# Two-layer hybrid trunk (DeltaNet and HGRN2 heads): one triangular inverse per layer instead of one per head pair, and the HGRN2 score levels in one step

## The chip, the cores and the metric

The kernel runs on one core of one Trainium2 chip, as one launch. The metric is the device time in microseconds (us); the time before is 1264.35 us, the median of three runs (1264.16 to 1266.21). One more run was taken with the profiler: its own time is 1263.9 us and its span, from the first to the last instruction of the program, is 1262.1 us. So 1.8 us lie outside the span, and the profiled run stands 0.45 us below the median.

The engines are named as in the profile: PE is TensorE, PEld its weight loads, DVE is VectorE, ACT is ScalarE, POOL is GpSimd, SP is SyncE, which here only issues DMAs.

## The reference

The model is a trunk of two layers over 256 tokens of width 2048. Each layer norms the residual h, multiplies it by one input matrix of 8208 columns, feeds two groups of heads, multiplies their joined output by an output matrix, and adds a gated per-layer embedding:

```python
for l in range(DEPTH):
    hn = rms_norm(h, norm_w[l])
    proj = hn @ w_in[l]
    y_a = deltanet_branch(dn_qkv, dn_z, dn_b, dn_a, ...)   # 8 heads of 128
    y_b = hgrn2_branch(hg_q, hg_f, hg_i, hg_z, ...)        # 8 heads of 128
    h = h + concatenate([y_a, y_b]) @ w_out[l]
    gate = sigmoid(h @ w_ple_gate[l])
    h = h + (p[l] @ w_ple_up[l]) * gate
return rms_norm(h, final_norm_w)
```

The DeltaNet branch solves, for every head and chunk, a unit lower triangular system, which the kernel does by forming the inverse:

```python
A = where(strict, einsum("bhncd,bhnsd->bhncs", k_beta, k) * decay, 0.0)
sol = triangular_solve(A + eye, rhs, left_side=True, lower=True, unit_diagonal=True)
```

The HGRN2 branch forms causal scores with a decay for each channel, `A = einsum("bhrd,bhsd,bhrsd->bhrs", q, k, exp(G_r - G_s))`, and multiplies them into the values. The result does not depend on the chunk length; the kernel works in chunks of 128 tokens, so a head has two chunks.

## The kernel before

**The large products.** Every matrix product of the trunk is made in three passes of rounded factors: `whi` by the high part of the activations, `wlo` by the high part, `whi` by the low part (`products`, L414). A weight piece of 512 KB is loaded on SP's queue into `raw`; `prep` (L387) rounds it on ACT to `whi` (L400) and subtracts on DVE to `wlo` (L402). One *step* (`run_step`, L436) multiplies one such piece: two K tiles, two token tiles and three passes, 12 PE matmuls with 512 moving columns. Three pieces of `raw` and three of `whi`/`wlo` are held, and pieces are prepared two steps ahead (`LOOK`).

**The stages.** A layer has three stages: `in` (17 chunks of up to 512 columns), `out` (4 chunks) and `gate` (4 chunks, with `up`). `in_order` (L61) gives the chunks of `in`: `kq` is the k and q columns of one pair of DeltaNet heads (group g of four), `vz` its v and gate columns, `fq` and `iz` the forget/query and value/gate columns of a pair of HGRN2 heads. The first two chunks of a stage are taken alternately. `OUT_KTS` (L72) is the order in which `out` reads the eight results `y` (two K tiles each: 0 to 7 are DeltaNet, 8 to 15 HGRN2).

**The small work.** The heads' own work is written as generators, which are spawned when their chunk of `in` is finished. After every step `tick` (L358) counts all of them down by one; a generator that yields a number goes on that many steps later. The numbers stand in `DELAY` and `DELAY_AT` (L38 to L54): for instance `t16` 2 means that the next group of small matmuls stands two steps further on. All PE instructions keep the order in which they are written (`PEOrder`, L334), so a small matmul whose operand is late stops the large products behind it. The instructions of the other engines are ordered by a scheduler of the framework from the order of the text and the free buffers; a few DVE instructions and DMAs are pinned too.

**DeltaNet, per pair of heads (`DN`, L612).** A pair has four 128x128 matrices (two heads by two chunks). `dkdq` convolves k and q; `k_side` waits `k` steps; `q_side` waits `q` steps, makes the strict triangles `Bt` and the scores `QK` (L725 to L734), and then inverts its four matrices: it writes `Bt` to DRAM (L738), reads the 16x16 diagonal blocks back as `F` with one block to a partition, 32 partitions (L742), substitutes column by column with 30 DVE instructions (L752 to L757), writes the block inverses to the diagonal of the cleared DRAM array `d2` (L758), and reads the whole matrices back as `Tt` (L760). Three doublings follow, each with two groups of fp32 matmuls `pp` and `px`: from 16 to 32 in 64x64 blocks (L767 to L785), from 32 to 64 in 32x32 blocks (L787 to L806), from 64 to 128 in 64x64 blocks (L808 to L825). `dv` waits for this inverse (L841) and then runs a chain of small groups `pz`, `pS`, `pw`, `pz`, `po`, one step apart.

**HGRN2, per pair of heads (`HG`, L890).** The scores of a chunk are put together from levels: at level u a block of u rows meets the u columns ahead of it, with factors in which the decay is split at the block's edge (`factors`, L955). The levels go out in four groups of matmuls, three steps apart: level 1 with the diagonal and level 2 (called A below), 4 and 8 (B), 16 and 32 (C), 64 and the product of the two chunks, 128 (D). `place` (L988) merges the levels into the score tile by predicated copies.

Of the kernel before, what the change touches and what calls it, by code (L numbers as in the profile page):

```python
# [31 lines left out]
def chunk_cols(chunk):  # L32
# [6 lines left out]
    "d": {'c': 1, 'D': 4, 'k': 5, 'q': 5, 'ssq': 1, 'F': 3, 'T': 9, 't16': 2, 'p16': 2, 't32': 2, 'p32': 2, 't64': 2, 'p64': 2, 'v': 5, 'z0': 1, 'S': 1, 'w': 1, 'z1': 1, 'o': 1, 'y': 3, 'yp': 1},  # L39
    "b": {'o': 1, 'g': 4},  # L40
    "h": {'c': 1, 'f': 1, 'a': 4, 'u1': 3, 'u4': 3, 'u16': 3, 'o': 2, 'y': 2, 'yp': 1, 'q': 0},
# [30 lines left out]
OUT_KTS = (0, 1, 2, 3, 4, 5, 8, 9, 10, 11, 6, 7, 12, 13, 14, 15)  # L72
# [75 lines left out]
def const_arrays():  # L148
    i = np.arange(128)
    c = np.zeros((128, 4 * 128 + 256 + 32), np.float32)  # L150
    c[:, 0:128] = np.eye(128)
    c[:, 128:256] = 1.0
    c[:, 256:384] = i[:, None] > i[None, :]
    c[:, 384:512] = i[:, None] <= i[None, :]
    c[:, 512:768] = (np.arange(256) % 128 != 0)[None, :]
    c[:, 768:800] = i[:, None] % 32 == np.arange(32)[None, :]
    s, r = i[:, None], i[None, :]
    m = np.zeros((128, NMASK), np.int32)
    m[:, 0:32] = (s % 64 // 32 == np.arange(32)[None, :] // 16) & (s % 32 < 16)
# [7 lines left out]
def trunk(ctx: ExitStack, tc: tile.TileContext, head, xT, x, pT, W, par, fw, cst, msk, eye, out):  # L167
# [19 lines left out]
    cs = cp.tile([128, 800], F32, name="cs")  # L187
    ms = cp.tile([128, NMASK], I32, name="ms")

    def first(out, in_):  # L190
# [4 lines left out]
    xt = [mp.tile([128, 1024 if k else 1024 + NNW], F32, tag="et" if k < 2 else "kq", name=f"xt{k}", bufs=2)  # L195
          for k in range(4)]
# [73 lines left out]
    ident, ones, SL, UI = (cs[:, 128 * j:128 * j + 128] for j in range(4))  # L270
    keep, ident32 = cs[:, 512:768], cs[:, 768:800]
# [8 lines left out]
    d2 = dr.tile([66048], F32, name="d2")  # L280
    dfull = lambda d: d.rearrange("(i x) -> i x", i=4)[:, 0:16384].rearrange("i (p c) -> p i c", c=128)
    ddiag = lambda d: d.rearrange("(q x) -> q x", q=32)[:, 0:2048].rearrange("q (s f) -> q s f", s=16)[:, :, 0:16]
# [4 lines left out]
    def clear_scratch():  # L287
        V.tensor_copy(SLr, SL)
# [5 lines left out]
        tc.keep_in_program_order(nc.scalar.dma_start(out=dfull(d2), in_=zero.rearrange("p (i c) -> p i c", i=4)))  # L294
# [181 lines left out]
    def small(tag, n=4):  # L476
        return sp.tile([128, n], F32, tag=tag, name=tag)
# [133 lines left out]

    class DN:  # L612


        def __init__(self, l, g, row, y):
            self.l, self.g, self.row, self.y = l, g, row, y
# [13 lines left out]
        def decay(self):  # L630
# [17 lines left out]
            self.eG, self.neG = small("eG", 2), small("neG", 2)  # L648
# [20 lines left out]
        def conv_silu_kq(self, ps, which, w):  # L669
            ac, sg = self.conv(ps, which)  # L670
            for hh in range(2):
                V.tensor_tensor(self.kq[:, hh, :, w, :], v4(ac[:, 256 * hh:256 * hh + 256]),
                                v4(sg[:, 256 * hh:256 * hh + 256]), ALU.mult)

        def stat(self, w, name):

            ps = pm.tile([128, 512], F32, tag="m", name=self.n + name)
            for i in range(4):
                PE.transpose(ps[:, 128 * i:128 * i + 128], self.kq[:, i // 2, i % 2, w, :], ident)
# [6 lines left out]
        def dkdq(self, ps, c0):  # L686
# [4 lines left out]
            self.kq = mix("kq", 1024, 2, n + "kq").rearrange("p (h t w c) -> p h t w c", h=2, t=2, w=2)  # L691
# [5 lines left out]
        def k_side(self):  # L697
# [4 lines left out]
            self.ktail = mix("ktail", 256, 1, n + "kt")  # L702
# [4 lines left out]
            self.invn = small("invn")  # L707
            S.activation(self.invn, lk, AF.Exp, scale=0.5)
            self.b, self.nb = small("b"), small("nb")
# [6 lines left out]
        def q_side(self):  # L716
# [4 lines left out]
            Bt = self.Bt = v4(mix("Bt", 512, 1, n + "Bt"))  # L721
            self.QK = v4(mix("QK", 512, 2, n + "QK"))
            Dt = v4(self.Dt)
            for hh in range(2):
                pg = pm.tile([128, 512], F32, tag="m", name=n + f"pg{hh}")  # L725
                for t in range(2):
                    PE.matmul(pg[:, 256 * t:256 * t + 256], kq[:, hh, t, 0, :],
                              kq[:, hh, t, :, :].rearrange("p w c -> p (w c)"), start=True, stop=True)
# [10 lines left out]
            fx = tmp(n + "fx")[0:32].rearrange("q (w a b) -> q w a b", w=2, a=16)  # L739
            F, X = fx[:, 0], fx[:, 1]  # L740
            nc.scalar.dma_start(out=X, in_=eye)
            nc.scalar.dma_start(out=F, in_=ddiag(d1))  # L742
# [6 lines left out]
            self.nq = small("nq")  # L749
            S.activation(self.nq, lq, AF.Exp, scale=-0.5, bias=lnhd)  # L750
            yield self.wait("F")
# [598 lines left out]
```

## Time and profile before

| what | value |
|---|---|
| median of three runs | 1264.35 us (1264.16 to 1266.21) |
| profiled execution, its own time | 1263.9 us |
| its span | 1262.1 us |
| PE busy | 1248.5 us, 8001 matmul records |
| DVE busy | 923.6 us, 1752 instructions |
| ACT busy | 785.1 us, 1411 instructions |
| granted TensorE clock, mean | 0.997 |
| first large product starts, last one ends | 4.7 us, 1252.3 us |

An fp32 matmul stands in the trace as two records, a large product (rounded factors) as one. Because matmuls overlap in the array, a record's duration is longer than its share of the time: what a matmul costs the PE is read from the distance between starts. The timeline view merges a run of equal records into one row, which gives the start of the first.

### The profile page before, as it was taken

What the parts mean: (1) busy time and instruction counts of PE and PEld (TensorE: products, weight loads), DVE (VectorE), ACT (ScalarE), POOL (GpSimd) and SP (SyncE); (2) the same over time, 40 slices, a digit from 0 to 9 for tenths busy, and PEclk for the clock granted to TensorE, in tenths of its full rate; (3) what the DMA queues carried; (4) which work ended last, traced back from release to release, by engine and by line L of the source; (5) the groups of instructions that cost most, each with busy time, mean ns of one, the idle gap of its engine ahead of it and who ended that gap; (6) DMA issues with size and microseconds to landing.
All of it is one profiled execution on the core that took longest, in us unless ns stands there. A gap on an engine that the chain in (4) does not pass through costs nothing.

```text
span 1262.1 us, 21116 instructions
## 1 busy us (share of the span) xinstructions
PE 1248.5 (99%) x8001; PEld 1036.7 (82%) x8001; DVE 923.6 (73%) x1752; ACT 785.1 (62%) x1411; POOL 65.2 (5%) x57
## 2 busy tenths in 40 slices
PE   9999999999999999999999999999999999999996
PEld 7988887888887888888888888878888888888886
DVE  7789679787796855547668886897877968565566
ACT  7667666666666754437557677667666766444465
POOL 0100010020000000000002000100100000000010
PEclk9999999999999999999999999999999999999998
DMA  8565545455555455555555555544555545655553
GB/s 285 189 229 169 176 155 174 130 168 177 162 173 163 139 177 182 190 191 186 183 188 169 173 169 164 169 145 135 180 182 176 169 142 175 184 184 184 184 200 134
DMA packets 78246, 220.90 MB, mean 175 GB/s; under 512 B 15680, under 2 KB 25280, under 8 KB 78144
## 3 DMA queue, kind: packets, MB, share of 16 engines
q1 hardware_dynamic: 59040, 211.65, 52.2%
q10 hardware_dynamic: 19104, 7.90, 2.3%
q8 instruction: 63, 1.03, 0.3%
q14 instruction: 39, 0.32, 0.1%
HBM read 214.80 MB, written 4.72 MB: 174 GB/s over the span
## 4 chain that ended last, share of the span: by engine, by line
PE 92%; DVE 5%; ACT 1%; issue 1%; DMA 0%; SPq 0%; ACTq 0%; DVEq 0%
PE out L336 14%; PE gate L336 13%; PE in1dk L336 7%; PE in0dk L336 7%; PE in1hf L336 6%; PE in0hf L336 6%; PE in0dv L336 6%; PE in1dv L336 6%; PE in1hi L336 5%; PE in0hi L336 5%; PE up L336 2%; DVE wlo L402 1%; PE in1dz L336 1%; PE in0dz L336 1%; ACT whi L400 1%
## 5 line engine op out<-in xcount | busy, mean ns | idle before, releaser
L402 DVE TENSOR_TENSOR wlo<-raw,whi 128x1024 fp32r<-128x1024 f32 (+1 forms) x392 | 479.1, 1225 | 246.7 <-ACT whi L400 244.8
L400 ACT ACTIVATE whi<-raw 128x1024 fp32r<-128x1024 f32 (+1 forms) x392 | 411.4, 1051 | 342.2 <-PE out L336 84.2
L336 PE MATMUL in1hf<-whi,n1hi 128*128 128x512 f32 x128 | 52.5, 410 | 0.0
L336 PE MATMUL in1hi<-whi,n1hi 128*128 128x512 f32 x128 | 51.5, 403 | 0.0
L336 PE MATMUL in1dk<-whi,n1hi 128*128 128x512 f32 x128 | 51.2, 400 | 0.0
L336 PE MATMUL in1dk<-wlo,n1hi 128*128 128x512 f32 x128 | 50.0, 391 | 0.2 <-DVE wlo L402 0.2
L336 PE MATMUL gate<-whi,g0hi 128*128 128x512 f32 x128 | 50.1, 392 | 0.0
L336 PE MATMUL in1hf<-whi,n1lo 128*128 128x512 f32 x128 | 50.1, 391 | 0.0
L336 PE MATMUL in1hi<-whi,n1lo 128*128 128x512 f32 x128 | 50.0, 390 | 0.0
L336 PE MATMUL in1hf<-wlo,n1hi 128*128 128x512 f32 x128 | 49.9, 390 | 0.0
L336 PE MATMUL in1hi<-wlo,n1hi 128*128 128x512 f32 x128 | 49.9, 390 | 0.0
L336 PE MATMUL in1dk<-whi,n1lo 128*128 128x512 f32 x128 | 49.9, 390 | 0.0
L336 PE MATMUL gate<-whi,g0lo 128*128 128x512 f32 x128 | 49.8, 389 | 0.0
L336 PE MATMUL gate<-wlo,g0hi 128*128 128x512 f32 x128 | 49.8, 389 | 0.0
L336 PE MATMUL in1dv<-whi,n1hi 128*128 128x512 f32 (+1 forms) x128 | 48.3, 378 | 0.0
L336 PE MATMUL in1dv<-wlo,n1hi 128*128 128x512 f32 (+1 forms) x128 | 46.7, 364 | 0.0
L336 PE MATMUL in1dv<-whi,n1lo 128*128 128x512 f32 (+1 forms) x128 | 46.5, 363 | 0.0
L336 PE MATMUL gate<-whi,g1hi 128*128 128x512 f32 (+1 forms) x120 | 45.5, 379 | 0.0
L336 PE MATMUL gate<-wlo,g1hi 128*128 128x512 f32 (+1 forms) x120 | 45.4, 379 | 0.0
L336 PE MATMUL gate<-whi,g1lo 128*128 128x512 f32 (+1 forms) x120 | 45.4, 378 | 0.0
L336 PE MATMUL in0hf<-whi,n0hi 128*128 128x512 f32 x96 | 39.2, 408 | 0.0
L336 PE MATMUL in0hi<-whi,n0hi 128*128 128x512 f32 x96 | 38.5, 401 | 0.0
(1596 smaller groups left out, 3245.0 us busy)
## 6 DMA issues: line engine op xcount, KB each, us to landing
raw<-W SPq DMA_DIRECT2D x384, 512.0 KB, 3.5
raw<-W SPq DMA_DIRECT2D x7, 544.0 KB, 3.9
h<-x SPq DMA_DIRECT2D x4, 512.0 KB, 5.9
xt<-xT SPq DMA_DIRECT2D x3, 512.0 KB, 6.2
out_dram<-h SPq DMA_DIRECT2D x6, 256.0 KB, 2.1
fw<-fw ACTq DMA_DIRECT2D x2, 512.0 KB, 5.1
pin<-pT ACTq DMA_DIRECT2D x2, 256.0 KB, 3.2
out_dram<-h ACTq DMA_DIRECT2D x2, 256.0 KB, 2.9
```

Source lines behind the costliest of these rows:

```text
L336: return tc.keep_in_program_order(nc.tensor.matmul(*a, **k))
L400: S.activation(hi[:, sl], raw[:, sl], AF.Copy)
L402: V.tensor_tensor(lo[:, sl], raw[:, sl], hi[:, sl].bitcast(F32), ALU.subtract)
```

## The change

- `DN.q_side` ends after the q norms; its inverse moves to a new class `Inverse`, of which a layer has one. Each pair writes its `Bt` into a quarter of one large tile and into DRAM; when the fourth pair has done so, all 16 matrices of the layer are inverted together: one read of the diagonal blocks (128 partitions), 30 DVE instructions, one write, one read back, and three doublings of two groups each. The first doubling works in 32x32 blocks with 16 moving columns, where it had 64x64 blocks with 32; the second keeps its blocks; the third has its stationary operand in two halves of 32 columns.
- `in_order` takes the four `kq` chunks first; `dv` and `vz` come after the third `fq`. `OUT_KTS` starts with HGRN2's results.
- HGRN2's levels 1 to 64 go out in one group, after `f2`, `f4` and `a` steps; level 128 follows in a group of its own.
- What must outlive its pair has more buffers (`ktail`, `QK`, `eG`, `invn`, `b`, `nq`); k and q are kept in two tiles, one for each chunk. Two tiles that were loaded into `kq` are loaded into the inverse's `Tt`. The clearing of `d2` is four DMAs instead of one. The delays are set anew.

```diff
@@ q_side
-            d1 = dr.tile([66048], F32, tag="dB", name=n + "d1", bufs=2)
-            nc.scalar.dma_start(out=dfull(d1), in_=Bt)
...
-            (the inverse of four matrices, moved and widened)
+            self.inv.given(self.g)
@@ class Inverse (new)
+        def given(self, g):
+            sl = slice(4 * g, 4 * g + 4)
+            nc.scalar.dma_start(out=dfull(self.d1)[:, sl], in_=self.Bt[:, sl])
+            self.have += 1
+            if self.have == NG:
+                spawn(self.run())
+        def run(self):
+            n, Bt, NT = self.n, self.Bt, self.NT          # NT = 16
+            fx = tmp(n + "fx").rearrange("q (w a b) -> q w a b", w=2, a=16)
+            F, X = fx[:, 0], fx[:, 1]
+            nc.scalar.dma_start(out=X, in_=eye)
+            nc.scalar.dma_start(out=F, in_=ddiag(self.d1))
+            yield self.wait("F")
+            for c in range(1, 16):
+                pr_ = sp.tile([128, 15, 15], F32, tag="prod", name=n + f"pr{c}", bufs=1)
+                i = V.tensor_tensor(pr_[:, :c, :c], X[:, :c, :c], bc1(F[:, :c, c], c), ALU.mult)
...
+                V.tensor_reduce(X[:, :c, c:c + 1], pr_[:, :c, :c], mybir.AxisListType.X, ALU.add)
+            nc.scalar.dma_start(out=ddiag(d2), in_=X)
+            Tt = self.Tt = v4(mix("Tt", 128 * NT, 1, n + "Tt"))
+            nc.scalar.dma_start(out=Tt, in_=dfull(d2))
+            yield self.wait("T")
+            blocks = range(0, 128, 32)
...
+            for b in blocks:
+                i = V.transpose(Tn[b:b + 32], Tt[b:b + 32, :, b:b + 32])
...
+            yield self.wait("t16")
+            for i in range(NT):
+                for b in blocks:
+                    PE.matmul(pp[b:b + 32, 16 * i:16 * i + 16], Bt[b:b + 32, i, b:b + 32], Tn[b:b + 32, i, 0:16],
+                              start=True, stop=True)
...
@@ dv
-            yield self.after("T")
+            yield lambda: self.inv.ready
@@ HG.q_side
             xs = factors((2,))
+            yield self.wait("f2")
+            xs += factors((4, 8))
+            yield self.wait("f4")
+            xs += factors((16, 32)) + factors((64,))
             yield self.wait("a")
...
+            products(UNITS[1:], xs, pa, 192)
...
+            place(UNITS, [w1[:, :, 32:48]] + [v16(pa[:, 192 + 64 * j:256 + 64 * j]) for j in range(4)])
...
+            xs = factors((128,))
+            yield self.wait("u64")
@@ in_order
-    return [(("dz", 0), ("ba", 0)), kq(0), (("dv", 0),), fq(0), kq(1), vz(1), iz(0), fq(1), kq(2), vz(2), iz(1),
-            kq(3), vz(3), fq(2), iz(2), fq(3), iz(3)]
+    return [(("dz", 0), ("ba", 0)), kq(0), kq(1), kq(2), kq(3), fq(0), iz(0), fq(1), iz(1), fq(2), (("dv", 0),), vz(1),
+            iz(2), vz(2), fq(3), vz(3), iz(3)]
-OUT_KTS = (0, 1, 2, 3, 4, 5, 8, 9, 10, 11, 6, 7, 12, 13, 14, 15)
+OUT_KTS = (8, 9, 10, 11, 0, 1, 2, 3, 12, 13, 4, 5, 6, 7, 14, 15)
@@ DELAY (new entries of the inverse and of HGRN2)
+    "i": {'F': 4, 'T': 10, 't16': 2, 'p16': 2, 't32': 2, 'p32': 2, 't64': 3, 'p64': 2},
+    "h": {'c': 1, 'f': 1, 'f2': 2, 'f4': 3, 'a': 3, 'u64': 1, 'o': 2, 'y': 2, 'yp': 1, 'q': 0},
@@ clear_scratch
+        for j in range(NG):
+            tc.keep_in_program_order(nc.scalar.dma_start(out=dfull(d2)[:, 4 * j:4 * j + 4], ...))
```

More of the change, by code (lines that the diff above doesn't have):

```diff
@@ L194, in trunk @@
     NNW = KT
[L195 to L196 removed]
+    xt = [mp.tile([128, 1024 if k else 1024 + NNW], F32, tag="et", name=f"xt{k}", bufs=2) for k in range(2)]
+    xt2 = mp.tile([128, 2048], F32, tag="Tt", name="xt2", bufs=1)
+    xt += [xt2[:, 0:1024], xt2[:, 1024:2048]]
     def xk(k, n=1):
@@ L758, in q_side @@
-            nc.scalar.dma_start(out=ddiag(d2), in_=X)
-            Tt = self.Tt = v4(mix("Tt", 512, 1, n + "Tt"))
-            nc.scalar.dma_start(out=Tt, in_=dfull(d2))
-            yield self.wait("T")
-            Tn = tmp(n + "T16")
-            tc.keep_in_program_order(V.transpose(Tn, Tt.rearrange("p a b -> p (a b)")))
-            yield self.wait("t16")
-            pp = pm.tile([128, 512], F32, tag="m", name=n + "pp16")
-            two = lambda ap: ap.rearrange("p (b c) -> p b c", b=2)
@@ L787, in q_side @@
-            Tn = tmp(n + "T32")
-            for b in (0, 64):
-                V.transpose(v4(Tn)[b:b + 32, :, 0:32], Tt[b:b + 32, :, b:b + 32])
-            yield self.wait("t32")
-            pp = pm.tile([128, 512], F32, tag="m", name=n + "pp32")
-            for i in range(4):
-                for b in (0, 64):
-                    PE.matmul(pp[b + 32:b + 64, 32 * i:32 * i + 32], Bt[b:b + 32, i, b + 32:b + 64],
-                              v4(Tn)[b:b + 32, i, 0:32], start=True, stop=True)
```

279 lines of the change are left out of this document (146 added, 133 removed), and 8 rows, old and new, of the table DELAY_AT.

## The prediction

> **What bounds the kernel now.** I read the busy table first, then the chain that ended last, then who waited for whom on PE.
>
> ```profile
> span 1262.1 us, 21116 instructions
> PE 1248.5 (99%) x8001; PEld 1036.7 (82%) x8001; DVE 923.6 (73%) x1752; ACT 785.1 (62%) x1411; POOL 65.2 (5%) x57
> ...
> PE 92%; DVE 5%; ACT 1%; issue 1%; DMA 0%; SPq 0%; ACTq 0%; DVEq 0%
> ```
>
> ```profile
> PE warm L336 <- DVE zeros L237: 1.1, 1, 1.1
> ...
> PE in1dk L336 <- DVE wlo L402: 0.2, 1, 0.2
> ```
>
> PE is busy for 99% of the span, and its waits are few and short (us in total, times, longest): the list ends at 0.2 us and its longest is 1.1. So the time is the length of PE's own stream with a start and a tail around it, and whatever shortens that stream without a new wait shortens the kernel by as much. DVE is no bound by its share; whether it is one for a while is a rival below.
>
> Since durations of matmuls overlap, I price by starts, in the timeline of PE (start us, us, then the group with its number of records). Six places show the small groups that the change touches, alone or side by side:
>
> ```profile
> 118.44 0.39 PE L336 MATMUL in0dv<-wlo,n0hi 128*128 128x512 f32 x1
> 118.67 0.39 PE L336 MATMUL in0dv<-whi,n0lo 128*128 128x512 f32 x1
> 118.99 0.71 PE L336 MATMUL hg00pa<-hg00X 128*32 128x16 f32 x48
> 119.63 0.50 PE L336 MATMUL in0dv<-whi,n0hi 128*128 128x512 f32 x1
> 119.96 0.40 PE L336 MATMUL in0dv<-wlo,n0hi 128*128 128x512 f32 x1
> ...
> 156.54 0.68 PE L336 MATMUL dn00pp<-dn00T,dn00Bt 64*64 64x64 f32 x8
> 157.15 0.50 PE L336 MATMUL in0hi<-whi,n0hi 128*128 128x512 f32 x1
> ...
> 211.62 0.44 PE L336 MATMUL dn01px<-dn01Tt,dn01P 32*32 32x32 f32 x16
> 211.99 0.50 PE L336 MATMUL in0dk<-whi,n0hi 128*128 128x512 f32 x1
> ...
> 227.09 0.61 PE L336 MATMUL dn01pz<-dn01R,dn01Tt 128*128 128x128 f32 x4
> 227.45 0.48 PE L336 MATMUL in0dv<-whi,n0hi 128*128 128x512 f32 x1
> ...
> 370.20 0.39 PE L336 MATMUL in0hi<-whi,n0lo 128*128 128x512 f32 x1
> 370.52 0.66 PE L336 MATMUL dn03pp<-dn03T,dn03Bt 64*64 64x32 f32 x16
> 371.11 0.55 PE L336 MATMUL hg02pa<-hg02q,hg02k 128*32 128x48 f32 x32
> 371.47 0.47 PE L336 MATMUL hg02pa<-hg02X 128*32 128x16 f32 x32
> 371.87 0.50 PE L336 MATMUL in0hi<-whi,n0hi 128*128 128x512 f32 x1
> ...
> 381.06 0.74 PE L336 MATMUL hg02pa<-hg02X 128*32 128x16 f32 x64
> 381.73 0.50 PE L336 MATMUL in0hf<-whi,n0ahi 128*128 128x512 f32 x1
> ...
> 400.98 1.28 PE L336 MATMUL hg02pa<-hg02X 128*32 128x64 f32 x20
> 402.01 0.48 PE L336 MATMUL in0hf<-whi,n0hi 128*128 128x512 f32 x1
> ```
>
> A large product follows another after 0.23 us (118.44 to 118.67). Leaving that stream costs 0.32 - 0.23 = 0.09 (118.67 to 118.99, the same at 370.20), and coming back 0.33 - 0.23 = 0.10 more at the second large product (119.63 to 119.96). So a **break** of the stream costs 0.19 us beside what stands in it. A group itself takes, from its start to the next row's: first doubling (64x64 blocks) 0.59; second (32x32) 0.37; third (64x64) 0.61; A 0.76; B 0.67; C 0.64; D 1.03; a group of four 128x128 records 0.36.
>
> **The change part by part.** *Paces of new groups.* The 64 records of B take 0.67 and the 32 of A's second half 0.40, so a 16-wide record is 0.27 / 32 = 8.4 ns and a group's end costs 0.13. With that end: 48-wide 0.36 / 32 = 11 ns, 32-wide (0.37 - 0.13) / 16 = 15 ns. D less the group of four and one end is 0.54 for 16 records 64 wide, 34 ns; if the change of tile form inside D costs another 0.09, it is 28. The inverse's third doubling will have D's form (two halves of 32 columns, 64 moving), so I use 31, and 28 and 34 for the range.
>
> *Inverse, per layer.* Before: each of four pairs runs two groups at each doubling, 4 x 2 x (0.59 + 0.37 + 0.61) = 12.6. After: 128 records in each group of the first doubling, 128 x 8.4 ns + 0.13 = 1.21; 64 in the second, 64 x 15 + 0.13 = 1.09; 64 in the third, 64 x 31 + 0.13 = 2.11; two groups each, 8.8. Saved 3.7.
>
> *HGRN2, per layer.* Before: 4 x (0.76 + 0.67 + 0.64 + 1.03) = 12.4. After: levels 1 to 64 are 32 x 11 + 128 x 8.4 + 16 x 15 + 16 x 31 ns + 0.13 = 2.30, level 128 is 0.36; 4 x 2.66 = 10.6. Saved 1.8.
>
> *Breaks.* I laid out both versions' generators as a table of steps (a tick after each step, the delays as given) and counted the steps with a small group before them: 163 before, 133 after. The table puts C of group 0 at step 36 and the first doubling of pair 3, with A of group 2 in the same step, at step 110, as the rows at 118.99 and 370.52 do. 30 breaks x 0.19 = 5.7.
>
> Sum: 2 x (3.7 + 1.8) + 5.7 = **16.7 us** less PE stream. With 34 and 28 ns it is 15.5 and 17.9 (2 x 64 + 4 x 16 records, two layers, 3 ns).
>
> The 16-wide pace is from 128x32 tiles; the 32x32 tiles of the new first doubling are not in the trace with four blocks. The nearest by shape, 15 ns for two blocks with 32 columns, is the dear end: 128 x 6.6 ns x 4 groups = 3.4 us of the gain. I take 8.4, because in C, whose tiles are all 128x32, the 16 records with two of four column groups in use cost (0.64 - 0.13 - 32 x 8.4 ns) / 16 = 15 ns as well: it is the unused half that costs, not the shape. [...]
>
> *DVE, ACT.* The substitution's 30 instructions run twice instead of eight times, on 128 partitions instead of 32. A transpose of 64 partitions lasts as long as one of 128:
>
> ```profile
> L809 DVE STREAM_TRANSPOSE dn00T<-dn00Tt x1: 704/704/704, 148.2 to 148.2; 64x512 f32<-64x512 f32 x1
> L764 DVE STREAM_TRANSPOSE dn00T<-dn00Tt x1: 705/705/705, 108.5 to 108.5; 128x512 f32<-128x512 f32 x1
> ```
>
> So DVE is relieved. That is worth nothing by itself, since PE does not wait for DVE; it pays only if DVE would have been late.
>
> *DMAs and their queue.* Diagonal blocks go out and come back as 2048 pieces of 64 B once a layer, where 512 went four times. The worst pair before (median us to landing; the first and last of the substitution's 15 reductions; the transpose that ends the wait):
>
> ```profile
> d<-dn02fx ACTq DMA_DIRECT2D x1, 32.0 KB, 3.4
> dn02Tt<-d ACTq DMA_DIRECT2D x1, 256.0 KB, 5.6
> L757 DVE TENSOR_REDUCE dn02fx<-dn02pr x15: 144/201/369, 255.3 to 275.5; 32x1 f32<-32x1 f32 x1, 32x2 f32<-32x4 f32 x1, 32x3 f32<-32x9 f32 x1, 32x4 f32<-32x16 f32 x1
> L764 DVE STREAM_TRANSPOSE dn02T<-dn02Tt x1: 703/703/703, 286.5 to 286.5; 128x512 f32<-128x512 f32 x1
> ```
>
> A step lasts (370.52 - 118.99) / 74 = 3.4 us. The new delays leave `T` 10 and `t16` 2 steps, 40.8 us, from the substitution's place to the first doubling. It needs 20.2 for the substitution at its slowest, 3.4 to 13.6 for the store (as before, or four times), 5.6 to 22.4 for the read back, and four transposes of 0.7: 32 to 59 us. For the middle I take 7 and 10, since a 32 KB store and a 256 KB read are mostly fixed cost (8 times the bytes, 1.6 times the time): 40.0, just inside. The read back waits in ACT's queue for the store to land; behind it stand the next `whi`, two steps (6.8 us) ahead of PE, so up to 6.8 costs nothing. If that cover is gone, a 13.6 us landing stops PE for 6.8 us a layer. Three more 256 KB clears run at the start on ACT's queue: by the 5.6 us of a transfer of this size 0 to 17 us of landing; nobody needs `d2` before the first store, some 40 steps on, so 0.
>
> *Order.* In the table the inverse is ready before step 73 and pair 0 first needs it at 87, 14 steps x 3.4 = 48 us later. The last DeltaNet result is there before step 135 and `out` needs it at 140; before, 132 and 137. `fw` now waits for `Tt`, free at `out`'s step 3, and is needed over 40 steps later: 0.
>
> Forecast: 1263.9 - 16.7 = 1247.2 for a profiled execution; the median stands 0.45 above the profiled one, so **1247.6**.
>
> **The rivals.**
>
> [...]
>
> *DVE falls behind.* The inverse's transposes and copies now meet the factors of HGRN2's groups 0 and 1, while wave after wave of `wlo` goes on. A stretch before shows DVE full:
>
> ```profile
> 83.00:115.00 32.00, 32.00 (x271) 26.33 (x270) 31.69 (x71) 20.37 (x28) 0.00 (x0) 1.00 0.65 207
> ```
>
> (us, then busy PE, PEld, DVE, ACT, POOL.) DVE works 31.69 of 32 us and PE never stops. After, such a stretch lasts from step 46 to 73, 92 us, three times as long. If DVE falls behind by 5% there, 4.6 us a layer come back: 1247.6 + 9.2 = 1256.8. Against it: DVE's sum falls.
>
> *The inverse comes late: slower.* PE's order is fixed, so the first doubling's matmuls, standing before step 61, hold up every large product behind them until `Tt` is back and transposed. The gain of 8.4 us a layer is used up when the path takes 40.8 + 8.4 = 49 us; with landings near the dear end, 54 us, PE stands 13.2 a layer: 1247.6 + 26.4 = 1274.0. For it: 59 is in the bounds, and the slack of pair 2 before (substitution's end 275.5, transposes 286.5, 11 us with 9.0 of landings in it) is thin. Against it: 64 B pieces spread over 16 engines, and the scheduler may do the substitution sooner than at its slowest, as nothing else in the inverse waits then.
>
> *The old waits go too.* What the sums above leave out, a few tenths where two groups stand in one step, could vanish with the groups; at 0.2 for each of 30, 6 us: 1241.6.
>
> **How the numbers follow.** Forecast as worked, 0.53; blocks not side by side 0.17; DVE behind 0.14; late inverse 0.07; old waits gone 0.09. The likeliest's own range, 28 to 34 ns and a few small waits, is 1245 to 1250. The range for 8 in 10 takes in the old waits at its low end and DVE behind at its high end, 1240 to 1257, and leaves out the late inverse. Within 0.2% (2.5 us, what a measurement of this kernel can tell from no change) means 1261.9 to 1266.9: it takes the late inverse or DVE at about twice the price, 0.04. Slower: most of the late inverse, 0.06. Faster 0.90.
>
> **What would show it.** Right: PE still at 99%, 133 breaks, groups of 128 records in 32x32 tiles lasting about 1.2 us and of 192 to 200 HGRN2 records about 2.3; DVE's busy time down by tens of us. [...] DVE behind: waits of PE for `wlo` between steps 46 and 73. Late inverse: PE waits for the transposes ahead of the first doubling, or ACT's `whi` waits for the store. The forecast is wrong if PE's waits sum to more than 5 us, or if the large products' pace is no longer 0.23 us.

## The result and the profile after

The changed kernel takes 1280.23 us (median of 4 runs, 1277.91 to 1283.68) against 1264.26 us for the kernel before in the same session (4 runs): a ratio of 1.0125, 95% interval 1.0098 to 1.0152. It is 16 us slower, where the forecast was 16.7 us faster. The profiled execution took 1277.91 us.

From the page of the changed kernel, its span, the busy times and the engines' shares of the chain that ended last:

```profile
span 1276.1 us, 21612 instructions
PE 1239.2 (97%) x8385; PEld 1038.9 (81%) x8385; DVE 881.2 (69%) x1520; ACT 780.9 (61%) x1383; POOL 67.7 (5%) x57
...
PE 81%; DVE 9%; issue 3%; ACT 3%; DMA 3%; SPq 0%; ACTq 0%; DVEq 0%
```

PE's busy time fell by 9 us and DVE's by 42, as the prediction wanted, and yet the span grew by 14. Who PE waited for (us in total, times, longest):

```profile
PE hg11pa L339 <- issue: 3.4, 1, 3.4
PE di1pp L339 <- DVE di1T L690: 2.8, 2, 2.3
PE hg03pa L339 <- issue: 2.7, 1, 2.7
PE hg02pa L339 <- issue: 2.3, 1, 2.3
PE hg00pa L339 <- issue: 2.3, 1, 2.3
PE hg12pa L339 <- issue: 2.0, 1, 2.0
PE hg10pa L339 <- issue: 1.9, 1, 1.9
PE in0hi L339 <- DVE wlo L405: 1.8, 2, 1.3
PE hg00yp L342 <- DVE hg00yt L578: 1.3, 1, 1.3
PE in1hi L339 <- DVE wlo L405: 1.3, 1, 1.3
```

Before, the longest wait was 1.1 us and the list ended at 0.2. Now six of the eight merged HGRN2 groups stand still once, for 1.9 to 3.4 us, with "issue" as the releaser: no engine and no transfer that the profile shows. PE's timeline has such a group, the two groups of the first doubling, and a merged group that runs through:

```profile
179.48 0.55 PE L339 MATMUL hg00pa<-hg00q,hg00k 128*32 128x48 f32 x32
179.85 1.24 PE L339 MATMUL hg00pa<-hg00X 128*32 128x16 f32 x120
183.39 1.47 PE L339 MATMUL hg00pa<-hg00X 128*32 128x16 f32 x39 [2.30 <-issue]
...
206.83 1.26 PE L339 MATMUL di0pp<-di0T,di0Bt 32*32 32x16 f32 x128
209.38 1.02 PE L342 MATMUL hg00yp<-cs,hg00yt 128*128 128x128 f32 x4 [1.29 <-DVE hg00yt L578]
...
218.31 1.26 PE L339 MATMUL di0px<-di0Tt,di0P 32*32 32x16 f32 x128
219.50 0.50 PE L339 MATMUL in0hi<-whi,n0hi 128*128 128x512 f32 x1
...
239.56 0.55 PE L339 MATMUL hg01pa<-hg01q,hg01k 128*32 128x48 f32 x32
239.93 1.93 PE L339 MATMUL hg01pa<-hg01X 128*32 128x16 f32 x160
241.79 0.50 PE L339 MATMUL in0hf<-whi,n0ahi 128*128 128x512 f32 x1
```

From its start to the next row's, the unstalled group takes 241.79 - 239.56 = 2.23 us (2.30 was forecast), the 128 records of the first doubling 219.50 - 218.31 = 1.19 (1.21 was forecast). The stream is as cheap as forecast; what is new stands between its pieces. One more loss is in the PEclk column (us, then busy PE, PEld, DVE, ACT, POOL, PEclk, DMA share, GB/s):

```profile
180.00:190.00 10.00, 7.70 (x183) 6.54 (x170) 8.30 (x26) 4.24 (x9) 1.79 (x1) 0.83 0.36 108
870.00:880.00 10.00, 6.83 (x53) 5.27 (x55) 3.42 (x11) 2.69 (x8) 1.26 (x1) 0.66 0.44 143
```

Full speed is 1.00. The granted clock is 0.5 for 3.41 or 6.83 us from 183.1, 210.5, 811.2, 852.2 and 872.6 us, each time behind a stall or a wait of PE; before, never between the start and the tail.

So I split every profiled span into four: PE's idle stretches over 0.15 us that another engine ends ("waits"), those that nothing shown ends ("issue"), the time lost to half clock outside them, and the rest, which is the stream. For before 1262.1 = 3.6 + 0 + 0 + 1258.5; for after 1276.1 = 12.4 + 14.6 + 9.8 + 1239.2. The stream is 19.3 us shorter, and 33.3 us of stalls, waits and half clock are new. The experiments in one table (time and ratio are medians of several runs, the other columns are of the profiled one, which can stand some us off the median: with one delay of layer 1 changed it took 1266.8 against 1261.8; all in us):

| kernel | time | ratio to before, 95% | waits | issue | half clock | rest |
|---|---|---|---|---|---|---|
| before | 1264.3 | | 3.6 | 0.0 | 0.0 | 1258.5 |
| after | 1280.2 | 1.0098 to 1.0152 | 12.4 | 14.6 | 9.8 | 1239.2 |
| shifted edges | 1265.9 | 1.0003 to 1.0021 | 17.7 | 1.2 | 1.7 | 1241.6 |
| before, shifted | 1265.0 | 0.9997 to 1.0016 | 3.6 | 0.0 | 0.0 | 1259.8 |
| groups split | 1278.5 | 1.0082 to 1.0128 | 22.7 | 0.8 | 8.4 | 1245.5 |
| inverse and order alone | 1268.3 | 1.0021 to 1.0050 | 15.0 | 0.0 | 3.2 | 1248.4 |
| levels alone | 1292.0 | 1.0191 to 1.0245 | 19.6 | 7.4 | 7.5 | 1255.0 |
| other delays | 1276.7 | 1.0071 to 1.0134 | 13.5 | 12.8 | 10.2 | 1240.0 |
| other delays, shifted | 1271.3 | 1.0039 to 1.0082 | 18.2 | 2.8 | 5.1 | 1242.1 |
| shifted, GpSimd | 1282.7 | 1.0135 to 1.0165 | 30.0 | 1.0 | 9.4 | 1241.4 |
| shifted, GpSimd, store 2 steps on | 1287.2 | 1.0168 to 1.0202 | 28.3 | 2.9 | 10.0 | 1240.7 |
| the same, not shifted | 1299.2 | 1.0263 to 1.0300 | 26.4 | 15.0 | 16.0 | 1239.1 |
| shifted, GpSimd, store 4 steps on | 1266.5 | 1.0006 to 1.0025 | 16.3 | 1.4 | 6.5 | 1240.9 |
| inverse and order alone, GpSimd | 1289.8 | 1.0186 to 1.0220 | 32.6 | 0.0 | 12.0 | 1246.0 |
| the same, store 2 steps on | 1278.9 | 1.0094 to 1.0136 | 21.7 | 0.0 | 10.2 | 1247.2 |
| the same, store 4 steps on | 1268.7 | 1.0026 to 1.0055 | 16.0 | 0.0 | 5.0 | 1245.9 |
| shifted, outer products on DVE | 1264.7 | 0.9994 to 1.0013 | 16.9 | 0.8 | 5.1 | 1240.4 |
| and one delay of layer 1 | 1261.8 | 0.9972 to 0.9992 | 16.9 | 0.6 | 6.4 | 1241.1 |
| and level 128's factors earlier | 1260.0 | 0.9956 to 0.9981 | 12.1 | 0.8 | 3.4 | 1241.9 |

### The profile page after: what moved, and what is told of

It reads as the page before. It is cut to its first block, busy times and chain, and to the rows that moved or that the text cites. A ratio compares the mean times of both kernels' runs of the same rounds, so it can differ in the third digit from the quotient of the medians.

```text
span 1276.1 us, 21612 instructions
## 1 busy us (share of the span) xinstructions
PE 1239.2 (97%) x8385; PEld 1038.9 (81%) x8385; DVE 881.2 (69%) x1520; ACT 780.9 (61%) x1383; POOL 67.7 (5%) x57
## 3 DMA queue, kind: packets, MB, share of 16 engines
q8 instruction: 66, 1.08, 0.4%
## 4 chain that ended last, share of the span: by engine, by line
PE 81%; DVE 9%; issue 3%; ACT 3%; DMA 3%; SPq 0%; ACTq 0%; DVEq 0%
PE out L339 14%; PE gate L339 13%; PE in1hf L339 7%; PE in1dk L339 6%; PE in0hf L339 5%; PE in1hi L339 5%; PE in0hi L339 5%; PE in0dv L339 5%; PE in1dv L339 5%; DVE wlo L405 3%; PE in0dk L339 2%; PE up L339 2%; ACT whi L403 1%; DMA raw<-W 1%; PE in1dz L339 1%
## 5 line engine op out<-in xcount | busy, mean ns | idle before, releaser
L339 PE MATMUL in0hi<-wlo,n0hi 128*128 128x512 f32 x96 | 37.7, 393 | 1.8 <-DVE wlo L405 1.8
```

The source lines that it names most:

```text
L339: return tc.keep_in_program_order(nc.tensor.matmul(*a, **k))
```

## Experiments on the stalls

My theory: a small fp32 matmul is two records and four instructions of PE (two weight loads, two products), so a merged group of 192 records is 384 instructions in about 2.2 us. The page of after shows the instruction queue with 66 transfers and 1.08 MB, 16 KB each, one for every 254 of PE's 16770 records (before 63 for 16002, 254 too), and all six stalls begin 193 or 194 instructions into a block of 256, counted from the program's start. The rival: a late operation, a PSUM bank or a read that the trace doesn't name.

**Shifted edges.** Nothing but the place of the block edges changes:

```diff
         begun = warm(NWARM // 2)
+        zf = zeros.bitcast(F32)
+        for j in range(32):
+            b = 32 * (j % 4)
+            PE.matmul(warm_ps[b:b + 32, 0:16], zf[:, 0:32], zf[:, 0:16], start=True, stop=True)
```

> The changed kernel with 32 more small matmuls (128 instructions of PE) behind the warm-up, at a time when PE waits for its first operands anyway; nothing else is changed, so every edge between blocks of 256 instructions falls 128 instructions earlier in the rest of the program. Theory (instruction supply): the distance from a merged group's start to the edge becomes 177, 138, 183, 243 (layer 0, groups 0 to 3) and 228, 189, 234, 38 (layer 1) where it was 49, 10, 55, 115, 100, 61, 106, 166. The six groups that stalled lose their stalls, group 3 of layer 1, which had none, gets one of 2 to 3 us, and group 1 of layer 0 at most a short one: about 1260 us (1256 to 1266). Rival (the stall belongs to what these groups read, write or wait for): the same six groups stall by the same 1.9 to 3.4 us: 1277 to 1284.

Measured 1265.85 us, 14.4 less than the changed kernel. The six stalls are gone. Two new ones stand where they were foretold: 0.7 us in group 3 of layer 1, where 2 to 3 were expected, and 0.5 in the products behind group 1 of layer 0. The group of the row above now runs through, and its level 128 waits instead (PE's timeline with shifted edges):

```profile
179.55 0.55 PE L343 MATMUL hg00pa<-hg00q,hg00k 128*32 128x48 f32 x32
179.92 1.97 PE L343 MATMUL hg00pa<-hg00X 128*32 128x16 f32 x160
181.82 0.50 PE L343 MATMUL in0hf<-whi,n0hi 128*128 128x512 f32 x1
...
190.13 0.68 PE L343 MATMUL hg00pa<-hg00X 128*128 128x128 f32 x4 [2.55 <-DVE hg00X L1023]
```

**The same in the kernel before.**

> The kernel before with the same 32 small matmuls at the start. Its longest small group has 40 matmuls, 160 instructions, so no whole block lies in one. Theory: no change, 1264 +- 2. Rival (the extra matmuls help by themselves, for example by a warmer clock at the start): 1250 or so, as much faster as the shift made the changed kernel.

1264.98 us, interval 0.9997 to 1.0016: no change. The extra matmuls don't help by themselves.

**Dose.** In the kernel before, groups of N small matmuls stand ahead of 15 of the 16 chunks of `out` and `gate`, each at a chosen distance o, the number of instructions from the group's start to the next block edge:

```diff
+        for _ in range(pad):
+            PE.matmul(ps, zeros, zeros.unsqueeze(1).to_broadcast([128, 4, 128]), start=True, stop=True)
+        for j in range(n):
+            b = 32 * (j % 4)
+            PE.matmul(ps[b:b + 32, 0:16], zf[:, 0:32], zf[:, 0:16], start=True, stop=True)
```

> The kernel before with 15 groups of N matmuls of 32 columns and 16 moving in the out and gate stages, each ahead of the first product of an output chunk, into the bank that this product then clears; 128 x 512 products of zeros ahead of each group set the distance o from its start to the next edge between blocks of 256 instructions (a small matmul is 4 instructions). No group waits for another engine. Layer 0: N = 96 at o = 10, 50, 91, 130, 170, 210, 250, then N = 32 at 50; layer 1, o = 50: N = 64, 72, 80, 128, 192, 48, then N = 96 at 115. Theory (the next block is asked for at an edge and takes about 3.6 us, while 256 dense instructions take 1.1): a stall of about 2.5 us at the second edge for o of 10 to 115, of 2 to 2.5 in the first products behind the group at 130, none at 170, 210 and 250; none for N = 32, 48 and 64, some 0.5 us for 72, about 2.5 for 80, 128, two stalls for 192. The time is longer than before by what is added, some 260 us of products of zeros. Rival (small groups run freely, the stalls had another cause): no gap without a releaser anywhere.

1561.92 us (one run), 298 more than before, of which the 1069 products of zeros at 0.23 us each are 246. Two groups in PE's timeline, N = 96 at o = 50 and N = 192 at o = 51:

```profile
474.87 0.73 PE L347 MATMUL out<-zeros 128*32 128x16 f32 x39 [2.28 <-issue]
...
1399.56 1.87 PE L347 MATMUL gate<-zeros 128*32 128x16 f32 x128 [2.27 <-issue]
1403.58 1.58 PE L347 MATMUL gate<-zeros 128*32 128x16 f32 x102 [2.15 <-issue]
```

| N | o | stall, us | at instruction |
|---|---|---|---|
| 96 | 10 | none | |
| 96 | 50, 91, 115 | 2.28, 2.52, 2.21 | 306, 348, 372 |
| 96 | 130 | 1.52 | 386, in the products behind |
| 96 | 170, 210, 250 | none | |
| 32, 48, 64, 72 | 50 or 51 | none | |
| 80, 128 | 51 | 2.23, 2.14 | 308 |
| 192 | 51 | 2.27 and 2.15 | 308 and 564 |

Each stall stands 256 or 257 instructions behind the first edge, and the long group has a second one 256 further on. No group waited for another engine. So in this run the stall came where a whole block, or at o = 130 all but two instructions of one, lay inside the group, and the block behind it wasn't there in time. Two of fifteen came out otherwise than foretold: o = 10 and N = 72 have none; and at o = 130 the stall is 1.52 us, where 2 to 2.5 were foretold.

The trace's record of the instruction queue shows the same from the other side. At each stall of this run a transfer of 16 KB starts 0.8 to 1.5 us behind the edge at which PE enters the block, and PE goes on 1.3 to 1.5 us after it has landed, 3.2 to 4.0 us behind that edge; a block of small matmuls is used up in 1.1. In the six stalls of the changed kernel PE goes on 1.3 to 1.5 us after a landing, too. At o = 10 the transfer had landed 2.8 us ahead of the first edge, and so had, by 0.4 us, that of the changed kernel's group 1 of layer 0, the other group with o = 10 that runs through; what lets a transfer start so early no run tested. The levels-only kernel (below) fits: inside its merged groups it stalls at o = 97, 21 and 85 (1.8, 1.3, 3.4 us), and at none of the five from 129 to 226, though 0.95 us stand in the products behind the one at 150.

**Groups split.**

```diff
-            products(UNITS[1:], xs, pa, 192)
+            products(UNITS[1:3], xs[:2], pa, 192)
+            yield 1
+            products(UNITS[3:], xs[2:4], pa, 320)
```

> The changed kernel, with the 192 records of each merged HGRN2 group put into two groups of 96, one step apart (A to level 2 of the 16-wide products, then levels 4 to 64 and so on; same products, same inverse, same order). Theory (PE runs out of instructions: a group of 192 records is 384 instructions, and when a whole block of 256 of them lies inside the dense stretch, the next block is not there in time): no stall inside a group any more, each group 1.1 to 1.4 us; the 14.6 us of the six stalls and some 7 us of half clock behind them go, 8 more breaks at 0.19 us cost 1.5: about 1260 us (1256 to 1264), with the waits for wlo, yt and the inverse still there. Rival (something the trace does not name, such as the PSUM bank, the SBUF reads of the six factors or a late DVE operation, holds the group): the stalls of 1.9 to 3.4 us stay inside one of the halves, and the time stays at 1277 to 1284.

The stalls went (issue 0.8 us in all), so the theory held for them, but the time stayed: 1278.47 us. Waits rose by 10.3 us; that the extra step moved HGRN2's next steps onto those of the inverse would explain it, and no run tested that. Taking the stalls away in this way bought other waits; only the shifted edges, which leave the order alone, show their price.

**One part alone.** The changed kernel with the old four groups of levels, and the kernel before, its inverse and its order, with levels 1 to 64 in one group:

```diff
-    "h": {'c': 1, 'f': 1, 'f2': 2, 'f4': 3, 'a': 3, 'u64': 1, 'o': 2, 'y': 2, 'yp': 1, 'q': 0},
+    "h": {'c': 1, 'f': 1, 'a': 4, 'u1': 3, 'u4': 3, 'u16': 3, 'o': 2, 'y': 2, 'yp': 1, 'q': 0},
...
-            products(UNITS[1:], xs, pa, 192)
+            nxt = factors((4, 8))
+            products((2,), xs, pa, 192)
...
+            products((4, 8), xs, pa)
...
+            products((16,), xs, pa)
```

(in the second kernel the other way round, with `f2` 2, `f4` 3, `a` 3 and `u64` 1)

> The changed kernel with the HGRN2 levels as before (four groups A, B, C, D a step or more apart): the new inverse and the new order alone. Theory: no stall without a releaser inside a small group; what is left of the loss are the waits for wlo, for the eviction of dn00kqet and for the inverse of layer 1. The inverse's part of the saving is 7.4 us and 22 or so breaks are fewer, 4 us; the waits without a stall sum to about 13 us at most: 1254 to 1266, middle 1259. Rival (the loss comes with the inverse and the new order, the stalls only show where it happens): 1270 or more.

> The kernel before with its own order and its inverse for each pair, and HGRN2 levels 1 to 64 in one group: the second part of the change alone. Theory (instruction supply): groups that have a whole block of 256 instructions inside stall for 2 to 3 us, about half of the eight, and the granted clock halves for 3.4 us behind some of them: the 3.6 us that the levels save and about 3 us for 16 fewer breaks are outweighed by 10 to 17 us: 1264 to 1275. Rival (the stalls come from the new inverse or order, for example late factors): no stalls, about 1258.

Inverse and order alone: 1268.32 us, between the two expectations: no stall, but 15.0 us of waits where I had allowed 13 at most. Levels alone: 1292.04, outside both expectations. Three groups stall, as the edges say, and once the products behind one (7.4 us together), and 7.5 us go to half clock; the 19.6 us of waits I had not foreseen. With the delays as given, each part by itself makes PE wait.

## Experiments on the waits

With the stalls away the change is still worth nothing: its stream is 17 us shorter than before and PE waits 14 us more. The stalls had hidden a part: after has 12.4 us of waits, with shifted edges 17.7.

**Other delays, without and with the shift.**

```diff
-    "h": {... 'f4': 3, 'a': 3, 'u64': 1, 'o': 2, 'y': 2, 'yp': 1, 'q': 0},
+    "h": {... 'f4': 3, 'a': 3, 'u64': 2, 'o': 1, 'y': 2, 'yp': 1, 'q': 0},
...
-    "i1p32": 3, "i1p64": 3, "i1t32": 1,
+    "i1T": 11, "i1p32": 2, "i1p64": 3, "i1t32": 1,
```

(and 1 more for `h0u64` and `h3u64`, 1 less for `h0o`)

> The changed kernel with other delays only: level 128 of HGRN2 one step later after the merged group (its results in the same step as before), and layer 1's inverse one step later from its read back to the second doubling. In the trace with the shifted block edges these were the waits for hg00X, hg10X, hg02X and hg12X (2.6, 2.5, 0.9, 0.9 us, level 128's factors, which DVE makes after placing the merged group's results) and for di1T (2.3). No edge between instruction blocks moves by more than a few instructions, so the six stalls stay. Theory (two losses, one behind the other: the stalls of the instruction supply hide most of the late factors): a little faster than the changed kernel, 1272 to 1280, since of these waits only that for di1T (2.3 to 2.8) is open there. Rival (late factors are the whole loss, the stalls are an effect of them): 1262 to 1268.

> The same delays together with the 32 small matmuls at the start that shift the block edges by 128 instructions. Theory: the waits for hg00X, hg10X, hg02X, hg12X and di1T of the run with shifted edges, 9.2 us together, go, and 1.7 us of half clock behind one of them: 1265.9 - 10.9 = 1255 us (1252 to 1260), faster than the kernel before. Rival (the waits move on to the next late operation, since DVE is full in these stretches): 1263 to 1267.

1276.65 and 1271.34 us. The first is as the theory has it. The second is above both ranges: level 128 no longer waits, but `wlo` (1.3), `hg10yt` (2.3), `dn00R` (1.5) and `dn10R` (1.4) do, and di1T waits as before. The waits moved on, as the rival says, and cost more than it allowed.

**The substitution on GpSimd.** With shifted edges, and in the kernel with inverse and order alone, the substitution's 15 pairs of instructions run on GpSimd, by outer products in place of DVE's row sums:

```diff
-                i = V.tensor_tensor(pr_[:, :c, :c], X[:, :c, :c], bc1(F[:, :c, c], c), ALU.mult)
-                V.tensor_reduce(X[:, :c, c:c + 1], pr_[:, :c, :c], mybir.AxisListType.X, ALU.add)
+                i = G.tensor_tensor(pr_, X[:, :c + 1, c:c + 1].to_broadcast([128, c + 1, r]),
+                                    bc1(F[:, c, c + 1:], c + 1), ALU.mult)
+                G.tensor_tensor(X[:, :c + 1, c + 1:], X[:, :c + 1, c + 1:], pr_, ALU.add)
```

> [...] DVE loses its 30 instructions a layer, which in the run with shifted edges stand among the placements and level 128's factors of HGRN2's group 0 from 170 to 189 us. Theory (what is left of the loss is DVE being late in these stretches): the waits for hg00X and hg10X (2.6, 2.5) and for di1T (2.3, with 1.7 of half clock behind it) go: 1265.9 - 9 = 1257 us (1254 to 1261). The waits for wlo at 166 and 222 us stay. Rival (the waits go to the next late operation, as they did with the later level 128): 1263 to 1268.

> The new inverse and order with HGRN2's levels as before (1268.3 us), and the substitution on GpSimd. Theory: the waits for di1T (3.7, with 3.4 of half clock behind it), di0T (1.1) and those of hg00pa and hg10pa for the substitution's row sums (1.0 each) go: 1268.3 - 9 = 1259 us (1256 to 1262), faster than the kernel before. Rival: the waits move on, 1266 or more.

1282.74 and 1289.79 us: both far off. GpSimd was done at 171.8 us, but the store of its result stood in ACT's queue from 161.9 on. ACT's timeline of the first:

```profile
161.26 0.61 ACT L477 ACTIVATE hg00qsg<-hg00qsg 128x512 f32<-128x512 f32 x1
171.85 0.37 ACTq L661 DMA_DIRECT2D d<-di0fx  x1
172.27 1.09 ACT L975 ACTIVATE hg00fsg<-hg00fsg,lb,oml 128x256 f32<-128x256 f32 x2 [10.39 <-POOL di0fx L660]
```

and PE's waits there:

```profile
PE in0hi L343 <- ACT whi L407: 7.0, 1, 7.0
PE in1hi L343 <- ACT whi L407: 6.7, 1, 6.7
```

A DMA issue that waited for its data held up ACT's arithmetic behind it, here for 10.39 us. The prediction said so of the read back ("behind it stand the next `whi`"); the store did the same. So I gave both a place of their own, two steps on and one more:

```diff
+            yield self.wait("s")
             tc.keep_in_program_order(nc.scalar.dma_start(out=ddiag(d2), in_=X))
...
+            yield self.wait("r")
             tc.keep_in_program_order(nc.scalar.dma_start(out=Tt, in_=dfull(d2)))
...
-    "i": {'F': 4, 'T': 10,
+    "i": {'F': 4, 's': 2, 'r': 1, 'T': 7,
```

> The run with the substitution on GpSimd, with the store of its result issued two steps later on ACT's queue and the read back one more step later (seven steps then stay to the transposes, the sum is as before). In the run without this GpSimd ended the substitution at 171.8 us, 17 us earlier than DVE had, but the store stood in ACT's queue from 161.9 on and held everything behind it for 10.4 us, whi and hg00fsg among it. Theory (the lateness is DVE's and ACT's queues, not the work): ACT doesn't stop, the waits for hg00X, hg10X and di1T go, those for wlo of 0.7 to 1.3 us stay (about 6 us in all): 1252 to 1259 us, middle 1255, faster than the kernel before. Rival (waits move on): 1262 or more.

> The new inverse and order with HGRN2's levels as before, the substitution on GpSimd, its store and read back later in the same way. Theory: ACT doesn't stop, and the waits for di1T and di0T go: 1268.3 - 8 = 1260 us (1256 to 1263). Rival: 1266 or more.

> The first of these two kernels without the 32 small matmuls at the start, so with the block edges where the changed kernel has them. Theory (two separate losses): the six stalls of about 2 us inside the merged groups come back, with half clock behind some: 12 to 20 us slower than the same kernel with shifted edges. Rival (the stalls needed a PE that runs late): as fast as with shifted edges.

1287.24, 1278.88 and 1299.20 us. The first two are misses for the theory: in the first the store still stood 5.5 us in ACT's queue, and the read back 3.5, and in the second ACT stood still for 7.5 us at the store. The third is what it foretold, 12.0 us more than the first: stalls (15.0) and half clock come on top of other waits. With `s` 4, `r` 2, `T` 4:

> The merged levels with shifted block edges and the substitution on GpSimd, the store of its result four steps after its start in the program and the read back two more steps later (four steps then stay to the transposes). With two steps the store was reached by ACT at 168.1 us while GpSimd ended at 173.3, and the read back at 175.2 waited for the store's landing until 178.7; ACT stood for 5.5 and 3.5 us. Two and one steps later (6.8 and 3.4 us) both should find their data. Theory (queues, not work): ACT doesn't stop; the waits for hg00X, hg10X and di1T are gone, those for wlo stay: 1252 to 1260 us, faster than before. Rival (what is left moves on to another late operation): 1263 or more.

> The new inverse and order with HGRN2's levels as before and the same placing of substitution, store and read back. Theory: 1256 to 1263 us, as ACT doesn't stop and the waits for di1T and di0T shrink. Rival: 1266 or more.

1266.48 and 1268.66 us: the rival won in both. ACT no longer stops at these issues, and in the first the waits for hg00X and hg10X are gone, but di1T's stayed and those for `wlo` doubled (2.4 and 2.5 us). DVE was not simply relieved: beside GpSimd, which works from 159.4 to 175.7 us, its products of 128 x 256 take 0.52 to 0.54 us instead of 0.42. Counted from the `wlo` at 156 us, the one that PE waits for at 167 us starts after 11.95 us, where it started after 10.86 with shifted edges alone; this is most of what its wait grew by (1.3 to 2.4 us). What a DVE without the substitution and without GpSimd beside it would bring, no run shows.

**Single places.** Back on DVE, the outer products alone, with shifted edges:

> The same outer products, on DVE. The number of its instructions is the same, the largest has 64 elements a partition where the row sums had 225; by the trace's 0.14 us at 1 element and 0.53 at 225 the 30 take 2 to 4 us less a layer. Theory: the waits shrink by about these 2 to 4 us where the substitution is in the way, 1261 to 1264. Rival: no change, 1266.

1264.72 us, 1.1 less than with row sums, where 2 to 4 were expected; the intervals of the two overlap, so it may be nothing. By now one wait had outlived every edit: di1T at layer 1's second doubling. DVE's timeline of the changed kernel shows why:

```profile
844.79 0.42 DVE L1046 TENSOR_TENSOR hg11q<-hg11G 128x256 f32<-128x256 f32 x1
...
846.14 0.90 DVE L685 COPY_PREDICATED di1Tt<-ms,di1px 32x256 f32<-32x256 int32 x2
847.05 0.43 DVE L1013 TENSOR_TENSOR hg11X<-hg11X,hg11k 128x256 f32<-128x256 f32 x1
847.40 0.42 DVE L1019 TENSOR_TENSOR hg11X<-hg11X,hg11q 128x256 f32<-128x256 f32 x1
847.83 0.91 DVE L685 COPY_PREDICATED di1Tt<-ms,di1px 32x256 f32<-32x256 int32 x2
848.77 1.43 DVE L690 STREAM_TRANSPOSE di1T<-di1Tt 32x512 f32<-32x512 f32 x2
```

The change gives this place one step (3.4 us, `i1t32` 1). Copies and transposes fill it with 0.90 + 0.91 + 1.43 = 3.2 us, and HGRN2's group 1 starts just ahead. I had read the wait as an inverse that comes late, and the edit above moved its read back, to no effect. So that delay alone, and then level 128's factors in front of the placements:

```diff
-    "i1p32": 3, "i1p64": 3, "i1t32": 1,
+    "i1p64": 3,
```

> The outer products on DVE with shifted block edges (1264.7 us), with one delay changed: in layer 1 the second doubling's first products stand two steps behind the transposes, as in layer 0, where they stood one step (3.4 us); the step after it is shortened, so that the rest stays. In all runs since the change PE waits there for di1T, 2.2 to 3.3 us, whatever was done to the inverse's store and read back: four predicated copies of 0.47 and two transposes of 0.7 fill the step, and HGRN2's group 1 starts on DVE just ahead of them. Theory: this wait (2.3 + 0.5) and 1.7 us of half clock behind it go, the rest stays: 1264.7 - 4 = 1261 us (1259 to 1263). Rival (DVE's lateness only moves on): 1264 to 1266.

```diff
+            xs = factors((128,))
             w1 = pa[:, :192].rearrange("p (i c) -> p i c", c=48)
...
-            xs = factors((128,))
             yield self.wait("u64")
```

> The same with level 128's factors made ahead of the placements of the merged group's results on DVE, where the change makes them behind. Theory: the waits for hg00X and hg10X (2.1 each), hg02X and hg12X (1.0 and 0.9) go or shrink to half, with 3.4 us of half clock behind the first two: 3 to 9 us less than the kernel without it, 1252 to 1258, faster than the kernel before. Rival (what is late next takes their place): no change against it.

1261.83 and 1259.98 us. The first hit. The second gained 1.9 us, with overlapping intervals, where 3 to 9 were expected: its waits for hg00X and the rest are gone, but `hg00yt`, `hg10yt`, `dn00R` and `dn10R` took up 0.8 to 0.9 each. PE's waits in the last kernel, the longest two kinds:

```profile
PE in1hi L343 <- DVE wlo L409: 2.5, 3, 1.3
PE in0hi L343 <- DVE wlo L409: 2.2, 2, 1.3
```

This version is 0.2 to 0.4% faster than the kernel before. Its 12.1 us of waits are 8.5 more than before's, and half clock takes 3.4: the stream would allow some 12 us more.

## Why the prediction was wrong, point by point

**The stream was right.** Forecast 16.7 us less; the rest column fell by 19.3, and by 16 to 18 in the shifted kernels with merged levels. The trace has 30 breaks fewer, as counted. Group prices, from start to next start: first doubling 1.19 for 1.21, second 1.13 for 1.09, third 1.91 for 2.11, merged levels 2.23 for 2.30, level 128 0.36 to 0.47 for 0.36. With the inverse and order alone the rest is 10 us shorter, with the levels too 16 to 19.

**The step that failed first: "A group itself takes, from its start to the next row's".** I priced groups of 128 and 192 records by the pace of 32 to 64. No group before was longer than some 160 instructions, so no row could show that PE's supply of instructions ends: 14.6 us, and there was no term for it. I bounded the price of the new tile form, and not that of the new length.

**The second: "1263.9 - 16.7 = 1247.2".** The sum takes full clock for granted, as the trace of before had it (0.997). Three of the six stalls and two of PE's waits for DVE are followed by half clock, 9.8 us in all. Here a wait's price is its length and up to 1.7 us (3.41 us at clock 0.5) for each window of half clock that follows.

**The third: "So DVE is relieved. That is worth nothing by itself".** True, but the rival "DVE falls behind" had a chance of 0.14 and a size of 9 us, and 9 to 14 us of new waits came, most of them for DVE. Its reason was wrong: I asked whether DVE's sum would keep up over 92 us. It does: DVE works 77.5 of the 92 us from 156 on. Of the rival's own sign, waits for `wlo` in that stretch, the changed kernel has 1.8 us in layer 0 and 1.3 in layer 1. What is late is single operations with too few steps: a burst of HGRN2's factors ahead of `wlo`, placements ahead of level 128's factors, one step for 3.2 us of work. In the changed kernel `wlo` at 167.31 us stands behind a burst of 6 us:

```profile
160.11 1.23 DVE L405 TENSOR_TENSOR wlo<-raw,whi 128x1024 fp32r<-128x1024 f32 x1 [1.31 <-ACT whi L403]
161.25 0.88 DVE L968 SCALAR_TENSOR_TENSOR hg00k<-hg00fe,oml,hg00fsg 128x256 f32<-128x256 f32 x2
...
167.31 1.22 DVE L405 TENSOR_TENSOR wlo<-raw,whi 128x1024 fp32r<-128x1024 f32 x1
```

**Rivals.** That the four blocks of the first doubling do not run side by side, to which the forecast gave a chance of 0.17, no run shows: its 128 records took 1.19 us, where the dear end of 15 ns a record makes 2.05. Whether two of them ever work at the same moment, this trace doesn't tell: a large product's 512 columns take 0.23 us, so 16 columns one after the other would take 7.2 ns, and a record took 8.3. "The inverse comes late" at the first doubling falls: no wait stands ahead of it in either layer. "Old waits go too" falls. The forecast's own mark, waits over 5 us, was passed five times over.

**What stays open.** Whether the last 8.5 us of waits can be had: with merged levels no edit made those for `wlo` shorter. And why the changed kernel's four runs differ by 6 us among themselves. The granted clock goes with it, 0.989 in the two shorter runs and 0.986 in the two longer, which is 14 us of their spans lost to the clock against 18; why the windows of half clock fall differently wasn't tested.

## What to carry to other kernels

Count instructions, not only durations: in the changed kernel stretches of small matmuls that held a whole block of 256 instructions stopped for the next one, for 1.9 to 3.4 us in six of eight groups, and where the blocks' edges fell decided 14 us without a line of the computation changed. When several small groups are merged, ask for each operand how many steps its engine has left and what stands ahead of it in that queue, DMA issues too; an engine's share of busy time doesn't answer this. And when a wait is taken away and the time stays, split the span into waits, stalls, clock and stream before looking for the next cause.

## What the runs showed of the hardware

**Instruction supply.** 256 instructions of small fp32 matmuls ran in about 1.1 us (128 records at 8.4 ns), and where the block behind had not come yet, PE stood 1.9 to 3.4 us in the changed kernel and 2.1 to 2.5 in the dose run. Large products, with two instructions in 0.23 us, waited for it only behind such a group (1.52 us at o = 130). The kernel before, whose longest group has 160 instructions, has no stall; the changed kernel has 14.6 us of them.

**The clock.** All windows of half clock in one trace lie on one grid of 3.41 us. Over 18 traces, 58 of the 59 windows of this grid in which PE stood idle for 55% or more (1.9 us) were followed by a window at half clock; of those with 15 to 45% idle, 22 of 177, and of the 26 in between, 6. In the changed kernel the stall of 2.30 us from 181.1 us, 2.05 of it inside one window, was followed by one; the stall of 2.73 us from 413.6 us, which lies across two windows, was not, and neither was one of 2.4 us at 411.7 us in the run with other delays.

**DVE beside GpSimd.** With GpSimd's substitution running, DVE's products of 128 x 256 took 0.52 to 0.54 us instead of 0.42 (with the store 2 steps on, from 162.8 to 168.6 us), and GpSimd's 30 instructions 13.5 to 15.0 us of busy time, where they took 9.3 to 9.5 in the two runs in which DVE worked only 2 of those 12 us.
